# Hybrid stream encoder, first mixer: three transposes moved from TensorE to VectorE's 32x32 squares and DRAM

## The chip, the cores and the metric

One core of one Trainium2 chip. The metric is the device time of one execution in microseconds (us). The kernel before takes 1324.58 us, the median of 3 runs (1324.56 to 1324.66).

## The reference

One inference step of a two-layer encoder on 256 prompt frames and 32 sample frames (288 columns together), model width 1024, float32. Each layer is SwiGLU, mixer, SwiGLU, each behind an RMS norm and added to the stream. Layer 0's mixer, which the change is about, has 8 HGRN2 heads and 8 stick-breaking heads of 128 channels:

```python
def _mixer_ab(h, w_in, lb, g_out, g_q, g_k, w_out, s0, k_past, v_past):
    qa, fa, va, ga, qb, kb, vb = jnp.split(h @ w_in, ..., axis=-1)
    f = lb + (1.0 - lb) * jax.nn.sigmoid(fa)
    o_a, s_new = _hgrn2(silu(qa), 1.0 - f, va, jnp.log(f), s0)
    o_a = _rms(o_a, g_out) * jax.nn.sigmoid(ga)
    ...
    o_b = _stick_breaking(qb, pos, kb, vb, pos)
    return concat(o_a, o_b) @ w_out, s_new, kb, vb
# HGRN2:          S_t = diag(f_t) S_{t-1} + k_t v_t^T,  o_t = S_t^T q_t
# stick-breaking: A[t,s] = sigmoid(z_ts) * prod_{s<j<t} (1 - sigmoid(z_tj)),  o = A v
```

Layer 1's mixer is a gMLP; it and the four SwiGLU blocks are the same in both kernels.

## The kernel before, in words

Activations lie with channels on partitions and the 288 frames as columns. The weights stream from DRAM in chunks of 1024 rows x 256 columns (`fetch`, line 193, issued by SyncE's queue three chunks ahead into 3 buffers). ScalarE rounds each chunk to its high part `wh` (line 220), VectorE takes the rest `wl` (line 221), both in pieces of two 128-row blocks, four pieces to a chunk, and TensorE multiplies each block three times (`wl`, `wh` by the low part, `wh` by the high part: lines 260 to 262), 48 products of 288 columns to a chunk. A chunk's pieces are made while the chunk before it is multiplied. Where a chunk is complete, VectorE takes it out of PSUM (`evac`, `evac_heads`, lines 307 to 318).

The mixer (`mixer_ab`) takes four pairs of heads, numbered 0 to 3; each has seven chunks, in the order f, q, v, g, bv, bk, bq (HGRN's decay, query, value and gate, then stick-breaking's value, key and query). Small work runs beside the chunks in two lanes of Python generators: `hgrn` for a pair starts behind its v chunk, `stick_keys` behind bk, `stick` behind bq. `tick`, called after each 128-row block of a chunk, gives each lane its rate of steps (`RATES`), and a step runs to the next `yield`. At the end of the four pairs two output chunks are multiplied, the lanes are drained, and the last blocks follow. The Python order is only what the framework's scheduler starts from: it writes out one fixed queue for each engine, and each engine then works its queue strictly in that order, waiting where an operand or a buffer is not there. So the place of an instruction in its queue is decided when the program is built.

`hgrn` first makes the decayed products for seven levels (1, 2, 4 to 64 frames). At each level `widen` (lines 616, 617) updates `E` and `Pp`, `products` (596 to 600) writes a `QK` buffer (2 of them), TensorE makes the scores (623 to 628) and `place` (633, 639, 645) puts them into `sc` and `SS`; each level needs the one before. Then the decayed keys `kd` (tile `tmp`, lines 676, 677) are turned to frames-on-partitions by TensorE (`to_tok`, lines 142, 144, tile `kt`), the states `S` and outputs `o` are multiplied (696 to 718), ScalarE sums the squares (720), GpSimd takes the power (134), ScalarE scales (731), TensorE turns the outputs back (`to_cols`, lines 158, 160, tile `oT`) and VectorE gates them (740). `stick` makes scores `zs`, `z`, sigmoids, a scan on VectorE (858), the weights `Bz`, and turns them by TensorE (872 for the sample, 883 in `turned` for the prompt) before they multiply the values (895 to 901, tile `ob`).

`to_rows` (line 168 and line 172) already exists: VectorE turns each 32x32 square (`STREAM_TRANSPOSE`), four DMAs write the squares to a DRAM tile in row order, and a further DMA reads them back turned. Before, it is used for v and bv alone.

Of the kernel before, what the change touches and what calls it, by code (L numbers as in the profile page):

```python
# [22 lines left out]
PAST = 256
# [12 lines left out]
S2 = 2 * TS  # L36
N2 = 2 * NT
# [56 lines left out]
class Net:  # L94
    PIECE = 2
    NORM_RATE = 0.17
    RATES = (0.65, 0.55)

    def __init__(self, tc, ctx, I, O):
        self.tc, self.nc, self.I, self.O = tc, tc.nc, I, O  # L100
        e = ctx.enter_context
        self.const = e(tc.tile_pool(name="const", bufs=1))
        self.wraw = e(tc.tile_pool(name="wraw", bufs=3))
        self.wspl = e(tc.tile_pool(name="wspl", bufs=4))
        self.acc = e(tc.tile_pool(name="acc", bufs=2, space=PSUM))
        self.misc = e(tc.tile_pool(name="misc", bufs=4, space=PSUM))
        self.nrm = e(tc.tile_pool(name="nrm", bufs=1))
        self.rows = e(tc.tile_pool(name="rows", bufs=2, space=bass.MemoryType.DRAM))
        self.stream, self.pos = [], 0
        self.raw, self.spl = {}, {}  # L110
        self.uid = 0
        self.ahead = None
        self.lanes = []
        self.lv = None
        self.nlane = Lane(self.NORM_RATE)
# [418 lines left out]
    def hgrn(self, p, pool, d):  # L534
# [3 lines left out]
        nc, I, O = self.nc, self.I, self.O  # L538
        tt, mul = nc.vector.tensor_tensor, ALU.mult
# [8 lines left out]
        for b in range(2):  # L548
            h = 2 * p + b
            for x in (f[:, TS * b:TS * b + TS], f[:, S2:].rearrange("p (w h t) -> p h w t", w=2, h=2)[:, b]):  # L550
                nc.vector.tensor_scalar(out=x, in0=x, scalar1=self.lbc[:, h:h + 1],
                                        scalar2=self.lb[:, h:h + 1], op0=mul, op1=ALU.add)
        k = T("k")
# [12 lines left out]
        vs = vt[:, 0]  # L566
# [113 lines left out]
        Sn = T("Sn", [P, 2, 2, P])  # L680
        kts = []
        for b in range(2):
            pk = self.to_tok(kd, b, "kt")
            kt = T("kt", [P, 2, P], 2)
            nc.scalar.copy(out=kt, in_=pk[:, :TP].rearrange("p (w c) -> p w c", c=P))
            if b == 0:
                for h in range(2):
                    r = slice(TS * h, TS * h + TS)
                    nc.scalar.copy(out=ktz[r, h], in_=pk[r, TP:TP + P])
            kts.append(kt)  # L690
            yield
        for b in range(2):
            kt = kts[b]
            pn = self.ps("S")
            for w, (x, y) in enumerate(((kt[:, 0], vw(b)[:, 0]), (kt[:, 1], vw(b)[:, 1]), (ktz[:, b], vs))):
                mm(pn[:, w * P:w * P + P], lhsT=x, rhs=y, start=True, stop=True)  # L696
# [7 lines left out]

        g = d["g"]
        nc.scalar.activation(out=g, in_=g, func=AF.Sigmoid)
        po = []
# [18 lines left out]
        yield  # L726
        yield
        for b in range(2):
            on = T("on", [P, 384])
            for w in range(3 - b):  # L730
                nc.scalar.activation(out=on[:, w * P:w * P + P], in_=po[b][:, w * P:w * P + P], func=AF.Copy,
                                     scale=rs[:, 3 * b + w:3 * b + w + 1])
            yield
            pt = self.to_cols("oT", b, on[:, :TP].rearrange("p (w c) -> p w c", c=P), on[:, TP:])
            parts = [(b, slice(TS, NT), pt[:, :TP])]
            if b == 0:
                parts += [(h, slice(0, TS), pt[:, TP + TS * h:TP + TS * h + TS]) for h in range(2)]
            for h, c, x in parts:
                go = self.gc["go"] + 2 * p + h
                nc.vector.scalar_tensor_tensor(out=g[:, h, c], in0=x, scalar=self.cols[:, go:go + 1],  # L740
                                               in1=g[:, h, c], op0=mul, op1=mul)
            yield
        self.put(2 * p, g)
# [59 lines left out]
    def stick(self, p, pool, d):  # L803
# [75 lines left out]

        def turned(b):  # L880
            pw = self.ps("wT")
            for i in range(3):
                nc.tensor.transpose(pw[:, i * P:i * P + P], B[b][:, i * P:i * P + P], self.ident)
            wT = T("wT", [P, 384])
            nc.scalar.copy(out=wT, in_=pw[:, :384])
            return wT

        wT = turned(0)
        yield
# [6 lines left out]
        store(slice(kk, kk + 2), slice(0, TS), po[:, 0:S2].rearrange("p (h t) -> p h t", h=2))  # L896
        yield
        for b in range(2):
            po = self.ps("ob")
            mm(po[:, 0:256], lhsT=vt[:, 1 + b], rhs=wT[:, 0:256], start=True, stop=False)  # L900
            mm(po[:, 128:256], lhsT=vt[:, 3 + b], rhs=wT[:, 256:384], start=False, stop=True)
            if b == 0:
                wT = turned(1)
            store(kk + b, slice(TS, NT), po[:, :TP])
            yield
# [476 lines left out]
```

## Time and profile before

| | |
|---|---|
| runs | 1324.58 us median (1324.56 to 1324.66) |
| the profiled execution | 1324.58 us by the clock of the runs; span from first to last instruction 1322.9 us |
| TensorE busy | 1317.1 us, 100% of the span |
| VectorE, ScalarE, GpSimd busy | 887.1, 661.7, 41.7 us (67%, 50%, 3%) |
| mean DMA | 166 GB/s, 219.83 MB |
| mixer of layer 0 | about 222 to 497 us of the span |

TensorE's busy time counts the tail of each product, so its share says that it is never long without work, not that each product is at its peak rate. The other engines have idle time all along; what they do matters where TensorE's queue waits for it.

### The profile page before, as it was taken

The numbers are of one execution on the slowest core, as the hardware profiler recorded it, in microseconds if no ns is written. First come the engines' busy times: TensorE is split into PE (matmuls) and PEld (weight loads), VectorE is DVE, ScalarE is ACT, GpSimd is POOL, SyncE is SP. The second block draws the span as 40 slices with busy tenths as digits, with TensorE's granted clock in tenths as the row PEclk, the third lists the DMA queues.
The fourth block names the chain that finished last, engine by engine and source line by source line (L and its number), as shares of the span: only waits on it lengthen the run. The fifth ranks groups of instructions, "written<-read, shape, count | busy, mean of one in ns | idle before, by whom it ended". The sixth has DMA issues, their size and how long they took to land.

```text
span 1322.9 us, 24562 instructions
## 1 busy us (share of the span) xinstructions
PE 1317.1 (100%) x9922; PEld 1310.3 (99%) x9922; DVE 887.1 (67%) x1706; ACT 661.7 (50%) x1355; POOL 41.7 (3%) x70
## 2 busy tenths in 40 slices
PE   9999999999999999999999999999999999999998
PEld 9999999999999999999999999999999999999998
DVE  7666556889898866666655756655567976666653
ACT  7544445464746465544444644444655446444432
POOL 1000000010101000000000000030000000000000
PEclk9999999999999999999999999999999999999999
DMA  9555455565565546555545555576544545555453
GB/s 283 178 176 168 150 175 173 157 182 159 168 170 170 140 134 200 161 178 166 157 153 174 165 179 165 161 183 188 169 152 138 167 147 160 173 166 171 152 152 84
DMA packets 254852, 219.83 MB, mean 166 GB/s; under 512 B 41233, under 2 KB 254018, under 8 KB 254738
## 3 DMA queue, kind: packets, MB, share of 16 engines
q1 hardware_dynamic: 253906, 216.32, 53.5%
q0 software_dynamic: 672, 1.77, 0.7%
q8 instruction: 78, 1.28, 0.4%
q10 hardware_dynamic: 160, 0.17, 0.1%
q14 instruction: 36, 0.29, 0.1%
HBM read 210.89 MB, written 7.34 MB: 165 GB/s over the span
## 4 chain that ended last, share of the span: by engine, by line
PE 97%; DVE 2%; ACT 0%; issue 0%; POOL 0%; DVEq 0%
PE acc L262 30%; PE acc L261 30%; PE acc L260 30%; PE sc L623 1%; DVE wl L221 1%; PE sp L1082 1%; PE S L696 0%; PE zs L833 0%; PE acc L1157 0%; PE sc L651 0%; PE ob L900 0%; PE vt L988 0%; PE acc L280 0%; PE z L845 0%; PE ob L895 0%
## 5 line engine op out<-in xcount | busy, mean ns | idle before, releaser
L220 ACT CAST wh<-wraw 128x512 fp32r<-128x512 f32 x768 | 440.5, 619 | 490.3 <-PE acc L262 370.1
L221 DVE TENSOR_TENSOR wl<-wraw,wh 128x512 fp32r<-128x512 f32 x768 | 507.4, 688 | 253.4 <-ACT wh L220 252.9
L260 PE MATMUL acc<-xh,wl 128*128 128x288 f32 x2096 | 627.2, 299 | 0.0
L261 PE MATMUL acc<-xl,wh 128*128 128x288 f32 x2096 | 619.4, 295 | 0.0
L262 PE MATMUL acc<-xh,wh 128*128 128x288 f32 x2096 | 618.9, 295 | 0.0
L261 PEld LDWEIGHTS acc<-xl,wh 128*128 128x128 f32 x2096 | 394.1, 188 | 0.6
L260 PEld LDWEIGHTS acc<-xh,wl 128*128 128x128 f32 x2096 | 393.9, 188 | 0.4
L262 PEld LDWEIGHTS acc<-xh,wh 128*128 128x128 f32 x2096 | 393.6, 188 | 0.2
L260 PE MATMUL acc<-hh,wl 128*128 128x288 f32 x960 | 284.5, 297 | 0.0
L261 PE MATMUL acc<-hl,wh 128*128 128x288 f32 x960 | 283.4, 295 | 0.0
L262 PE MATMUL acc<-hh,wh 128*128 128x288 f32 x960 | 282.8, 295 | 0.0
L260 PEld LDWEIGHTS acc<-hh,wl 128*128 128x128 f32 x960 | 180.2, 188 | 0.8 <-DVE xT L402 0.2
L261 PEld LDWEIGHTS acc<-hl,wh 128*128 128x128 f32 x960 | 180.3, 188 | 0.1
L262 PEld LDWEIGHTS acc<-hh,wh 128*128 128x128 f32 x960 | 180.3, 188 | 0.0
L309 DVE TENSOR_TENSOR u<-acc,rb 128x576 f32<-128x576 f32 x52 | 39.3, 757 | 48.8 <-PE acc L262 48.8
L309 DVE TENSOR_TENSOR g<-acc,rb 128x576 f32<-128x576 f32 x47 | 35.6, 757 | 47.0 <-PE acc L262 47.0
L329 ACT CAST hh<-u 128x576 fp32r<-128x576 f32 x52 | 35.1, 675 | 58.4 <-DVE u L455 40.3
L330 DVE TENSOR_TENSOR hl<-u,hh 128x576 fp32r<-128x576 f32 x52 | 39.4, 758 | 7.1 <-ACT hh L329 1.3
L336 ACT ACTIVATE xh<-xT,cols 128x288 fp32r<-128x288 f32 x40 | 21.2, 531 | 24.8 <-DVE xT L404 15.4
L455 DVE TENSOR_TENSOR u<-u,g 128x576 f32<-128x576 f32 x44 | 33.1, 752 | 0.0
L453 ACT ACTIVATE g<-g 128x576 f32<-128x576 f32 x44 | 30.0, 682 | 0.1
L404 DVE SCALAR_TENSOR_TENSOR xT<-acc,xT 128x288 f32<-128x288 f32 x32 | 14.5, 455 | 17.0 <-PE acc L262 17.0
(303 smaller groups left out, 759.1 us busy)
## 6 DMA issues: line engine op xcount, KB each, us to landing
wraw<-in_ffn_w_up_dram SPq DMA_DIRECT2D x44, 1024.0 KB, 5.9
wraw<-in_ffn_w_gate_dram SPq DMA_DIRECT2D x43, 1024.0 KB, 5.4
wraw<-in_ffn_w_down_dram SPq DMA_DIRECT2D x32, 1024.0 KB, 5.7
wraw<-in_ab_w_in_dram SPq DMA_DIRECT2D x28, 1024.0 KB, 5.0
wraw<-in_c_w_in_dram SPq DMA_DIRECT2D x16, 1024.0 KB, 5.5
wraw<-in_ffn_w_down_dram SPq DMA_DIRECT2D x16, 768.0 KB, 4.6
wraw<-in_c_w_out_dram SPq DMA_DIRECT2D x8, 1024.0 KB, 5.6
wraw<-in_ab_w_out_dram SPq DMA_DIRECT2D x8, 768.0 KB, 5.2
```

The lines of the kernel that those rows point to most:

```text
L220: self.nc.scalar.copy(out=h[:, x], in_=w[:, a:b])
L221: self.nc.vector.tensor_tensor(out=l[:, x], in0=w[:, a:b], in1=h[:, x].bitcast(F32), op=ALU.subtract)
L260: mm(o, lhsT=l[:, k, c], rhs=hi[:, r], start=st, stop=False)
L261: mm(o, lhsT=h[:, k, c], rhs=lo[:, r], start=False, stop=False)
L262: mm(o, lhsT=h[:, k, c], rhs=hi[:, r], start=False, stop=en)
L309: self.nc.vector.tensor_tensor(out=x, in0=acc[:, :, :NT], in1=self.rb, op=ALU.mult)
L329: nc.scalar.copy(out=hh, in_=h)
L330: nc.vector.tensor_tensor(out=self.hl[:, k:k + 2], in0=h, in1=hh.bitcast(F32), op=ALU.subtract)
L336: nc.scalar.activation(out=self.xh[:, k], in_=x, func=AF.Copy, scale=g)
L404: nc.vector.scalar_tensor_tensor(out=x, in0=acc[b][:, :NT], scalar=scale, in1=x, op0=ALU.mult, op1=ALU.add)
L453: nc.scalar.activation(out=g, in_=g, func=AF.Silu)
L455: nc.vector.tensor_tensor(out=u, in0=u, in1=g, op=ALU.mult)
```

## The change

Everything is in layer 0's mixer.

- `hgrn`: the decayed keys `kd` go through `to_rows` (one VectorE transpose of 576 columns, four writes) and come back by one read into `kt` and two into `ktz`, in place of five TensorE transposes and four ScalarE copies for each pair. Seven `yield`s stand between the issue and the first use. The sigmoid of the gate moves ahead of them.
- `hgrn`: the prompt's normalised outputs go through `to_rows` (512 columns) and come back into the buffer of `vt`; the sample's part keeps one TensorE transpose, so four fewer for each pair. Seven more `yield`s stand before the gating.
- `stick`: the prompt's weights of both heads go through `to_rows` (384 columns each, turned in the key buffer `kn`) and come back into `wT` and into the buffer `pk` of the past keys, in place of six TensorE transposes and two ScalarE copies for each pair. Seven more `yield`s.
- The decay's floor, `lb + (1 - lb) * sigmoid`, four operations for each pair, moves from VectorE to ScalarE (line 551).
- DRAM row tiles: 6 buffers in place of 2. Lane rates: 0.85 and 0.62 in place of 0.65 and 0.55.

```diff
-    RATES = (0.65, 0.55)
+    RATES = (0.85, 0.62)
...
-        self.rows = e(tc.tile_pool(name="rows", bufs=2, space=bass.MemoryType.DRAM))
+        self.rows = e(tc.tile_pool(name="rows", bufs=6, space=bass.MemoryType.DRAM))
...
-                nc.vector.tensor_scalar(out=x, in0=x, scalar1=self.lbc[:, h:h + 1],
-                                        scalar2=self.lb[:, h:h + 1], op0=mul, op1=ALU.add)
+                nc.scalar.activation(out=x, in_=x, func=AF.Identity, scale=self.lbc[:, h:h + 1],
+                                     bias=self.lb[:, h:h + 1])
...
-        kts = []
-        for b in range(2):
-            pk = self.to_tok(kd, b, "kt")
-            kt = T("kt", [P, 2, P], 2)
-            nc.scalar.copy(out=kt, in_=pk[:, :TP].rearrange("p (w c) -> p w c", c=P))
...
+        kt = T("kt", [P, 4, P])
+        rows = self.to_rows(T("QK", [P, S2 + N2], 2)[:, 0:N2], [(0, kd)])
+        nc.sync.dma_start(out=kt, in_=rows[S2:].rearrange("(i t) c -> t i c", t=P))
+        for h in range(2):
+            r = slice(TS * h, TS * h + TS)
+            nc.sync.dma_start(out=ktz[r, h], in_=rows[r])
+        g = d["g"]
+        nc.scalar.activation(out=g, in_=g, func=AF.Sigmoid)
+        for _ in range(7):
+            yield
...
-            pt = self.to_cols("oT", b, on[:, :TP].rearrange("p (w c) -> p w c", c=P), on[:, TP:])
...
+        rows = self.to_rows(T("QK", [P, S2 + N2], 2)[:, 0:4 * P], [(0, on)])
+        ot = T("vt", [P, 5, P])
+        nc.sync.dma_start(out=ot[:, 0:4], in_=rows.rearrange("(i c) t -> c i t", c=P))
+        yield
+        pt = self.ps("oT")
+        nc.tensor.transpose(pt[:, 0:P], os, self.ident)
...
+        for _ in range(7):
+            yield
+        for h in range(2):
+            gated(h, slice(TS, NT), ot[:, 2 * h:2 * h + 2].rearrange("p w t -> p (w t)"))
...
-        wT = turned(0)
+        wTs = []
+        y = T("kn", [P, 2 * (PAST + NT)])
+        for b in range(2):
+            wT = T(("wT", "pk")[b], ([P, 384], [P, 2, PAST])[b])
+            wT = wT if b == 0 else wT.rearrange("p h s -> p (h s)")[:, 0:384]
+            rows = self.to_rows(y[:, 384 * b:384 * b + 384], [(0, B[b])])
+            nc.sync.dma_start(out=wT.rearrange("p (i t) -> p i t", t=P), in_=rows.rearrange("(i s) t -> s i t", s=P))
+            wTs.append(wT)
...
-        yield
+        for _ in range(7):
+            yield
         for b in range(2):
             po = self.ps("ob")
+            wT = wTs[b]
             mm(po[:, 0:256], lhsT=vt[:, 1 + b], rhs=wT[:, 0:256], start=True, stop=False)
             mm(po[:, 128:256], lhsT=vt[:, 3 + b], rhs=wT[:, 256:384], start=False, stop=True)
-            if b == 0:
-                wT = turned(1)
```

The change also moves instructions in the queues that the scheduler writes. Three places, where numbers tell tiles of one name apart, `acc` is a chunk's sum in PSUM, `wl` and `wh` are a chunk's low and high part, and `E`, `f`, `QK`, `sc`, `SS` belong to the levels of `hgrn`.

VectorE, from the end of pair 1's bq chunk to the first piece of pair 2's f chunk (`wl_4006` before, `wl_3902` in the change). Before:

```order
L781 TENSOR_SCALAR ks_3936<-kms_3935 128x5
L221 TENSOR_TENSOR wl_4006<-wraw_3768,wh_4005 128x512
L317 TENSOR_TENSOR bq_3993<-acc_3866,rb_2579 128x2x2x128
L786 SCALAR_TENSOR_TENSOR bkt_3899<-kt_3937,pw_3987,gk_2528 128x128 x3
L318 TENSOR_TENSOR bq_3993<-acc_3866,rb_2579 128x64
L786 SCALAR_TENSOR_TENSOR bkt_3899<-kt_3962,pw_3987,gk_2528 128x128 x2
L221 TENSOR_TENSOR wl_4006<-wraw_3768,wh_4005 128x512
```

There the levels of pair 1 are over when bq is taken out, and a piece of the next chunk stands ahead of it. In the change the queue goes on like this behind bq (the first rows, then the last):

```order
L317 TENSOR_TENSOR bq_4014<-acc_3892,rb_2579 128x2x2x128
L617 TENSOR_TENSOR f_3343<-f_3343 128x144x2
L596 TENSOR_TENSOR QK_3687<-k_3584,E_3591 128x40x4
L597 TENSOR_TENSOR QK_3687<-k_3584,E_3591 128x2x16x4
L598 TENSOR_TENSOR QK_3687<-q_3449,f_3343 128x256
L600 TENSOR_TENSOR QK_3687<-q_3449,f_3343 128x8x4
L883 TENSOR_TENSOR hl_2511<-ob_3708,hh_2510 128x256
```

```order
L639 COPY_PREDICATED SS_2518<-ls,sc_3808 64x64
L616 TENSOR_TENSOR E_3591<-E_3591,f_3343 128x4x64
L673 TENSOR_TENSOR qz_2519<-q_3449,f_3343 128x2x32
L617 TENSOR_TENSOR f_3343<-f_3343 128x4x64
L676 TENSOR_TENSOR tmp_3886<-k_3584,E_3591 128x320
L674 TENSOR_TENSOR q_3449<-q_3449,f_3343 128x256
L677 TENSOR_TENSOR tmp_3886<-k_3584,E_3591 128x2x128
L221 TENSOR_TENSOR wl_3902<-wraw_3673,wh_3901 128x512
```

From bq up to and with the first `wl` for pair 2's f chunk there are 45 instructions (rows with x2 counted twice), and no piece of the f chunk stands ahead of them.

TensorE at the same place: `acc_3892` is pair 1's bq chunk, `acc_4017` pair 2's f chunk. Before, one level of pair 1 and what follows it:

```order
L262 MATMUL acc_3866<-xh,wh_3776 128x288
L623 MATMUL sc_3931<-QK_3857 128x128 x2
L142 MATMUL kt_3937<-ident,bk_3863 128x128 x2
L144 MATMUL kt_3937<-ident,bk_3863 128x128
L260 MATMUL acc_3866<-xh,wl_3828 128x288
L261 MATMUL acc_3866<-xl,wh_3827 128x288
L262 MATMUL acc_3866<-xh,wh_3827 128x288
L260 MATMUL acc_3866<-xh,wl_3828 128x288
```

The level's scores stand among products of a chunk there, 18 products to a level. In the change:

```order
L908 MATMUL ob_3708<-pk_3508,bvt_3110 128x128
L623 MATMUL sc_3738<-QK_3687 128x128 x2
L623 MATMUL sc_3773<-QK_3723 128x128 x2
L626 MATMUL sc_3773<-QK_3723 128x128
L623 MATMUL sc_3808<-QK_3753 128x128 x2
L628 MATMUL sc_3808<-QK_3753 128x64
L623 MATMUL sc_3834<-QK_3785 128x128 x2
L623 MATMUL sc_3865<-QK_3820 128x128 x2
L142 MATMUL kt_3965<-ident,bk_3889 128x128 x2
L144 MATMUL kt_3965<-ident,bk_3889 128x128
L142 MATMUL kt_3982<-ident,bk_3889 128x128 x2
L260 MATMUL acc_4017<-xh,wl_3902 128x288
```

Six levels of scores (the first, `sc_3704`, just ahead of the rows shown), the second head of pair 0's `ob` and pair 1's key transposes now stand in a row between the last product of one chunk and the first of the next, with no product between them.

ScalarE, pair 1's outputs `o` and their norm (`on`, `so`, `pw`), up to the copy that the sample's transpose `oT` reads. Before:

```order
L547 ACTIVATE f_4141<-f_4141 128x576
L720 ACTIVATE on_4098,so_4099<-o_4135 128x128
L825 ACTIVATE bq_3993<-bq_3993,cols 128x512
L819 ACTIVATE on_4119,qms_4120<-ss_4122 128x128 x2
L614 COPY E_4398<-f_4141 128x288
L819 ACTIVATE on_4119,qms_4120<-ss_4122 128x128
L819 ACTIVATE on_4119,qms_4120<-ss_4157 128x128
L220 CAST wh_4273<-wraw_3997 128x512
```

In the change, pair 2's outputs:

```order
L797 COPY kn_4774<-kn_4915 128x256
L824 ACTIVATE on_4943,qms_4944<-ss_4946 128x128
L830 ACTIVATE bq_4841<-bq_4841,cols 128x512
L824 ACTIVATE on_4943,qms_4944<-ss_4946 128x128
L556 ACTIVATE tmp_5240<-q_5103 128x576
L824 ACTIVATE on_4943,qms_4944<-ss_4946 128x128
L824 ACTIVATE on_4943,qms_4944<-ss_4970 128x128 x2
L220 CAST wh_5115<-wraw_4845 128x512
L731 ACTIVATE on_4982<-o_4905,pw_4960 128x128
L220 CAST wh_5115<-wraw_4845 128x512
L220 CAST wh_5176<-wraw_4845 128x512 x2
```

The last scaled copy (L731, formerly one of the first three behind the power) now stands behind the copies of `kn`, the squares of stick-breaking's query, the scaling of bq, the sigmoid of the next q and a piece of the next chunk.

## Rows read from the trace of the kernel before

**Rows 1.** The page: busy time by engine, granted TensorE clock in 40 slices.

```profile
PE 1317.1 (100%) x9922; PEld 1310.3 (99%) x9922; DVE 887.1 (67%) x1706; ACT 661.7 (50%) x1355; POOL 41.7 (3%) x70
...
PEclk9999999999999999999999999999999999999999
```

**Rows 2.** Windows: one half of a pair; us, busy time (instructions) by engine, clock, DMA.

```profile
252.00:283.00 31.00, 30.82 (x241) 30.09 (x240) 27.81 (x81) 14.43 (x47) 2.08 (x3) 1.00 0.45 133
```

**Rows 3.** TensorE in order of time: start, duration, line, tiles, shape, count.

```profile
482.29 0.30 PE L262 MATMUL acc<-hh,wh 128*128 128x288 f32 x1
482.42 0.49 PE L872 MATMUL wTs<-ident,Bsz 128*128 128x128 f32 x3
482.75 0.49 PE L883 MATMUL wT<-ident,Bz 128*128 128x128 f32 x3
482.99 0.38 PE L260 MATMUL acc<-hh,wl 128*128 128x288 f32 x1
483.21 0.30 PE L261 MATMUL acc<-hl,wh 128*128 128x288 f32 x1
```

**Rows 4.** VectorE's groups by shape: busy us, mean ns of one, idle before.

```profile
L221 DVE TENSOR_TENSOR wl<-wraw,wh 128x512 fp32r<-128x512 f32 x768 | 507.4, 688 | 253.4 <-ACT wh L220 252.9
L598 DVE TENSOR_TENSOR QK<-q,f 128x256 f32<-128x256 f32 x28 | 11.6, 413 | 0.0
L633 DVE COPY_PREDICATED sc<-lv,sc 128x256 f32<-128x256 uint8 x20 | 11.1, 557 | 0.4
L617 DVE TENSOR_TENSOR f<-f 128x288 f32<-128x288 f32 x20 | 9.2, 461 | 0.1
L858 DVE TENSOR_TENSOR_SCAN C<-C,cfr 128x384 f32<-128x384 f32 x8 | 8.6, 1073 | 0.1
L616 DVE TENSOR_TENSOR E<-E,f 128x288 f32<-128x288 f32 x16 | 7.2, 452 | 0.0
L597 DVE TENSOR_TENSOR QK<-k,E 128x128 f32<-128x128 f32 x24 | 6.8, 284 | 0.0
L596 DVE TENSOR_TENSOR QK<-k,E 128x160 f32<-128x160 f32 x16 | 5.2, 325 | 0.0
L639 DVE COPY_PREDICATED SS<-ls,sc 64x64 f32<-64x64 uint8 x20 | 4.5, 224 | 0.1
L858 DVE TENSOR_TENSOR_SCAN Cs<-Cs,cfr 64x288 f32<-64x288 f32 x4 | 3.0, 750 | 2.5 <-ACT Cs L836 2.5
L317 DVE TENSOR_TENSOR bq<-acc,rb 128x512 f32<-128x512 f32 x4 | 2.7, 677 | 0.0
```

**Rows 5.** The chain that ended last: start, us, engine, tile, line, instructions.

```profile
303.70 0.43 PE ob L900 x2
...
311.88 0.44 PE sc L623 x4
```

**Rows 6.** ScalarE's groups by shape, 222 to 500 us.

```profile
L731 ACT ACTIVATE on<-o,pw 128x128 f32<-128x128 f32 x20 | 6.1, 375 | 0.1
...
L720 ACT ACTIVATE on<-o 128x128 f32<-128x128 f32 x20 | 5.5, 274 | 10.3 <-PE o L718 9.4 <-PE o L714 0.6
...
L720 ACT ACTIVATION_READ_ACCUMULATOR on<-o 128x1 f32 x20 | 3.9, 194 | 0.0
...
L556 ACT ACTIVATE tmp<-q 128x576 f32<-128x576 f32 x4 | 2.8, 688 | 0.0
```

**Rows 7.** GpSimd's groups by shape: the power behind the sums of squares.

```profile
L134 POOL TENSOR_TENSOR pw<-oms,mhalf 128x5 f32<-128x5 f32 x4 | 5.1, 1268 | 45.0 <-DVE oms L724 45.0
```

**Rows 8.** DMA issues by line: count, KB each, median us from issue to landing.

```profile
rows<-QK SPq DMA_DIRECT2D x16, 80.0 KB, 2.1
vt<-rows SPq DMA_DIRECT2D x4, 320.0 KB, 4.6
```

**Rows 9.** TensorE in order of time at the start of the span.

```profile
1.16 3.36 PE L1157 MATMUL acc<-ones 128*128 128x128 f32 x14 [1.16 <-DVE ms L1168]
...
8.69 0.82 PE L1193 MATMUL x<-ident,xs 128*128 128x128 f32 x6
```

More of the change, by code (lines that the diff above doesn't have):

```diff
@@ L680, in hgrn @@
         Sn = T("Sn", [P, 2, 2, P])
-        kts = []
-        for b in range(2):
-            pk = self.to_tok(kd, b, "kt")
-            kt = T("kt", [P, 2, P], 2)
-            nc.scalar.copy(out=kt, in_=pk[:, :TP].rearrange("p (w c) -> p w c", c=P))
-            if b == 0:
[L687 to L690, printed above, removed]
+        kt = T("kt", [P, 4, P])
[7 more added lines that the diff above has]
+        for _ in range(7):
             yield
         for b in range(2):
-            kt = kts[b]
             pn = self.ps("S")
-            for w, (x, y) in enumerate(((kt[:, 0], vw(b)[:, 0]), (kt[:, 1], vw(b)[:, 1]), (ktz[:, b], vs))):
+            for w, (x, y) in enumerate(((kt[:, b], vw(b)[:, 0]), (kt[:, 2 + b], vw(b)[:, 1]), (ktz[:, b], vs))):
                 mm(pn[:, w * P:w * P + P], lhsT=x, rhs=y, start=True, stop=True)
@@ L703, in hgrn @@
             nc.sync.dma_start(out=o[0, 0, 2 * p:2 * p + 2].rearrange("h c d -> c h d"), in_=Sn[:, w])
-        g = d["g"]
-        nc.scalar.activation(out=g, in_=g, func=AF.Sigmoid)
         po = []
@@ L727, in hgrn @@
         yield
+        on, os = T("tmp")[:, 0:4 * P], T("on", [P, 384])[:, 0:P]
         for b in range(2):
-            on = T("on", [P, 384])
-            for w in range(3 - b):
-                nc.scalar.activation(out=on[:, w * P:w * P + P], in_=po[b][:, w * P:w * P + P], func=AF.Copy,
+            for w in range(2):
+                c = slice((2 * b + w) * P, (2 * b + w) * P + P)
+                nc.scalar.activation(out=on[:, c], in_=po[b][:, w * P:w * P + P], func=AF.Copy,
                                      scale=rs[:, 3 * b + w:3 * b + w + 1])
-            yield
-            pt = self.to_cols("oT", b, on[:, :TP].rearrange("p (w c) -> p w c", c=P), on[:, TP:])
[L735 to L741, printed above, removed]
-            yield
+        nc.scalar.activation(out=os, in_=po[0][:, TP:384], func=AF.Copy, scale=rs[:, 2:3])
+        rows = self.to_rows(T("QK", [P, S2 + N2], 2)[:, 0:4 * P], [(0, on)])
[4 more added lines that the diff above has]
+        nc.tensor.transpose(pt[:, 0:P], os, self.ident)
+        gated = lambda h, c, x: nc.vector.scalar_tensor_tensor(
+            out=g[:, h, c], in0=x, scalar=self.cols[:, self.gc["go"] + 2 * p + h:self.gc["go"] + 2 * p + h + 1],
+            in1=g[:, h, c], op0=mul, op1=mul)
+        for h in range(2):
+            gated(h, slice(0, TS), pt[:, TS * h:TS * h + TS])
+        for _ in range(7):
+            yield
+        for h in range(2):
+            gated(h, slice(TS, NT), ot[:, 2 * h:2 * h + 2].rearrange("p w t -> p (w t)"))
+        yield
         self.put(2 * p, g)
@@ L878, in store @@
             nc.vector.tensor_tensor(out=self.hl[:, k, t], in0=x, in1=self.hh[:, k, t].bitcast(F32), op=ALU.subtract)
[L880 to L886, printed above, removed]
-        wT = turned(0)
+        wTs = []
[6 more added lines that the diff above has]
+            wTs.append(wT)
         yield
@@ L896, in stick @@
         store(slice(kk, kk + 2), slice(0, TS), po[:, 0:S2].rearrange("p (h t) -> p h t", h=2))
-        yield
+        for _ in range(7):
+            yield
         for b in range(2):
             po = self.ps("ob")
+            wT = wTs[b]
             mm(po[:, 0:256], lhsT=vt[:, 1 + b], rhs=wT[:, 0:256], start=True, stop=False)
             mm(po[:, 128:256], lhsT=vt[:, 3 + b], rhs=wT[:, 256:384], start=False, stop=True)
-            if b == 0:
-                wT = turned(1)
             store(kk + b, slice(TS, NT), po[:, :TP])
```

## The prediction, made before the changed kernel was run

> **What bounds the kernel now.** I read the page first: TensorE is busy for 1317.1 of 1322.9 us and its granted clock is full in every slice [rows 1]. In the order of time its products follow each other without a hole: one product of 288 columns takes 0.13 us of its queue [rows 3]. So a microsecond of TensorE's work that goes is a microsecond gained, and a microsecond in which TensorE waits is lost. The windows come next, since they show who could make it wait: in this half of a pair VectorE is busy for 27.8 of 31 us, ScalarE for 14.4 [rows 2]. VectorE has 10% to spare there, and it makes the low part of the weights for every product.
>
> **What goes.** 64 transposes (16 a pair: 5 of the keys, 5 of the outputs, 6 of the weights, 15 net of the one that stays) become 4: 60 fewer. In the order of time six of them and the product behind them take 482.42 to 483.21, 0.79 us; less 0.13 for the product, 0.66 / 6 = 0.11 us each [rows 3]. 60 x 0.11 = **6.5 us** off the path, 0.5%. ScalarE's copies out of PSUM that go and VectorE's four floor operations a pair are off TensorE's path; I cost them at nothing.
>
> **What comes, off the path.** Four VectorE transposes a pair and 22 more DMA issues on SyncE's queue. A write of rows lands in 2.1 us, the read back in 4.6 [rows 8], so a round trip is about 7 us with its issues. In the new TensorE queue keys, outputs and weights are first used 12 us or more of products behind their issue, so I expect no wait for a landing before pair 3's last weights. The next weights stand behind these issues on the same queue, but are fetched three chunks, some 19 us, ahead.
>
> **What comes, on the path.** The rows of order decide: the queues are fixed, and the new ones no longer mix the levels of `hgrn` with the pieces of the weights.
>
> (a) Behind bq of pairs 1, 2 and 3. VectorE has 45 instructions from the taking out of bq up to the first `wl` of the next chunk. By shape [rows 4]: bq 0.68; five L616, three at 0.452 and two of 256 columns at 0.41 (as L598), 2.18; six L617, 2.66; the products of three levels, 0.325 + 0.284 + 0.413 and L600 at 0.22 (as the small L639), 3.73; of two levels, 0.98 each, 1.96; four L633, 2.23; five L639, 1.12; `hl` 0.41; the last four about 1.5; `wl` 0.69. Sum 17.2 us, all behind the last product of bq. TensorE has in that time six scores of 0.44, three smaller ones of 0.22, one `ob` of 0.65 [rows 5] and five transposes of 0.11: 4.5 us. It waits 12.7 us, three times: **38.1**.
>
> (b) bk is taken out ahead of the first `wl` of bq (0.68 + 0.22 + 0.69 = 1.6), and in front of bv stand a `place` and a `wl` behind a score (0.56 + 0.69 = 1.25) [rows 4]; three pairs: **8.5**.
>
> (c) The norm of the outputs. ScalarE's queue from o's first head to the copy that `oT` reads: five squares of 0.47, 2.3, with VectorE's mean 0.2 and the power 1.27 [rows 7], four scaled copies of 0.375, 1.5, three of `kn`, 1.1, five squares, 2.3, bq's scaling and q's sigmoid at 0.69, one `wh` at 0.69, the copy 0.375: 11.1 us [rows 6]. TensorE has 45 products, the rest of o and five transposes, 7.4 us. It waits 3.7. Then the sample's weights: power, two pieces, a scan of 0.75, a piece and four small operations on VectorE, some 4.9 us against 3.5 on TensorE, 1.4 more. Three pairs x 5.1 = 15.3; pair 3 has only 19 products to put between, wait 7.2 + 0.5 = 7.7. Sum **23.0**.
>
> (d) Pair 0's levels are still mixed with products, but with about 11 to a level, not 18: from the second to the last score VectorE has, by the same prices and with one `wl` and bv's taking out, 14.9 us, TensorE 65 products (8.6) and five scores (2.9), 11.5. It waits 3.4; bk, taken out behind that, comes 1.1 late by the same count: **4.5**.
>
> (e) The end. Between the sample's weights and the last blocks TensorE has 4.5 us; VectorE has two scans of 1.07 and their products and transposes, five pieces, the gating, then ScalarE's rounding: 9.5. Wait 5.0. The second weight round trip (two more issues and a read behind the first) adds 3.5: **8.5**.
>
> (f) A product's result comes about 0.16 us after its slot: the last three transposes end at 483.24, their slots at 483.08 [rows 3]. At some 20 such places: **3.4**.
>
> Waits 38.1 + 8.5 + 23.0 + 4.5 + 8.5 + 3.4 = 86.0; less 6.5: +79.5. The profiled execution took 1324.58 us, 1322.9 of it span, which is also the median of the runs; so 1324.6 + 79.5 = 1404.1, I say **1404**.
>
> Unseen operations. A transpose of 384 columns lies between nothing saved and the 0.69 of a `wl`; four floor operations on ScalarE between 0.2 and 0.69 each; both stand inside waits already counted or off the path, so between 0 and 2 us in all; I take 0, as they are nearest to work that is hidden now. A landing at 4.6 us rather than 2.1 moves (e) by 2.5.
>
> TensorE's clock, apart from this sum: at the start of the span 14 products of 128 columns take 3.36 us, 0.24 each, where four such passes take 0.44, 0.11 each, later; they follow 1.16 us of no work, and the close spacing is there at 8.69, six transposes in 0.82 [rows 5, 9]. So the lower level, 1.2 GHz by this spacing, is a state of this kernel too, at its start; from 8.69 on it is 2.4. The waits of (a) are the first long idleness of TensorE after that. The Trainium skill, "TensorE: Matmul & The Clock Gate", Part 1 (The HAM clock gate), says that an idle TensorE falls back to half rate and must be busy again before it gets the full one. The trace's start agrees, and no row shows a fall in the middle. By the rule the change would lose more than the waits; that is a rival below.
>
> **Rivals.**
> 1. The clock falls in each wait of (a). Price from the start: 1.16 to 8.69 at half rate loses 3.8 us; three times, 11: **1415**. For it: 12.7 us of waits with short scores only. Against: it may come back sooner, and what follows a wait may be held by VectorE anyway.
> 2. Only (a), (b) and (f) are waits, since in (c) to (e) ScalarE and VectorE run ahead in the idle time that (a) gives them: 38.1 + 8.5 + 3.4 - 6.5 = +43.5, **1368**. For it: they do work while TensorE stands. Against: the queues of (c) begin at o, which TensorE must first make.
> 3. SyncE becomes late. The load of the past keys into `pk` now waits for pair p's second `ob`, at the end of (a)'s start, and pv, the key rows and the next g chunk's weights stand behind it. If each pair's g chunk came 10 us late: +30, **1434**. It decides from the point where the 22 issues and their landings use up the 19 us of lead.
> 4. Not slower: VectorE reaches the levels early, while bq is multiplied, and only (b) and small waits stay, below the 6.5 us that are saved: **1318**. The place is (a): if bq's taking out did not stand ahead of the levels, or waits there came to under 2.2 us each. The rows of order speak against it, and nothing of the profile for it.
> 5. The edit does not do what it says: TensorE would still turn. Order shows 60 transposes fewer; I give it nothing.
>
> **How the numbers follow.** The forecast 0.45 (its own range 1388 to 1420, by 20% of the waits), rival 1 0.27, rival 2 0.15, rival 3 0.09, rival 4 0.04. 1365 to 1438 holds all but rival 4 and the half of rival 3 that goes beyond. 0.2% (2.6 us) is about what a measurement of this kernel can tell from no change. Slower 0.96, within 0.2% 0.01, faster 0.03.
>
> **What would show it.** In the new profile TensorE's sum of product groups is 6.5 us less and its idle time some 85 us more. The largest idle group stands before the first low product of a chunk, released by VectorE's `wl`, with three waits of about 13 us. Idle time before `oT` is put down to ScalarE's `on`, before `wTs` to VectorE's `Bsz`. If rival 1 holds, products behind the long waits stand twice as far apart, 0.27 us. If idle time before `S`, `ob` or the weights' pieces is put down to DMAs, rival 3 holds. The prediction is wrong if TensorE's waits before `wl` sum to under 25 us, or if the span grows by under 40.

## The result, and the profile after

The changed kernel takes 1385.45 us, the median of 4 runs (1385.08 to 1386.12), beside 1324.57 us for the kernel before on the same chip: ratio 1.046, 95% interval 1.0442 to 1.0478. It is slower by 60.9 us; the forecast was +79.5. 1385.45 lies inside the range of 1365 to 1438, and 2.6 us below the forecast's own of 1388 to 1420.

The page of the changed kernel answers to [rows 1]: 60 instructions of TensorE fewer, a span of 1383.4 us, and granted clock below full in some slices of the mixer.

```profile
span 1383.4 us, 24560 instructions
...
PE 1334.0 (96%) x9862; PEld 1318.4 (95%) x9862; DVE 892.8 (65%) x1706; ACT 660.4 (48%) x1347; POOL 43.6 (3%) x70
...
PEclk9999999999998988999999999999999999999999
```

By busy time TensorE's idle time grew by 43.6 us only (1383.4 - 1334.0 against 1322.9 - 1317.1), since a product at half rate counts as busy for longer. So I count otherwise: from the start of one TensorE instruction to the start of the next, less the slot that its kind takes in an undisturbed stretch (0.1325 us a product, 0.11 a transpose, other kinds likewise). In the mixer (222 to 560 us) that leaves 70.5 us of loss, where the kernel before has 3.0 (222 to 545). The difference, 67.4, less the 6.5 us of the 60 transposes is 60.9: the whole change of the time lies here.

Who ended TensorE's waits, over the whole span of the changed kernel (engine, tile and line that waited, who came last: us in all, times, longest):

```profile
PE acc L260 <- DVE wl L221: 12.8, 10, 3.2
PE sc L623 <- DVE QK L600: 9.5, 6, 1.9
PE ss L142 <- ACT tmp L729: 6.0, 4, 1.7
PE wTs L877 <- DVE Bsz L869: 4.3, 3, 1.5
PE acc L260 <- ACT hh L329: 3.9, 1, 3.9
PE sc L623 <- DVE SS L639: 3.7, 3, 1.2
PE sc L623 <- DVE QK L598: 2.7, 6, 0.6
...
```

The six groups left out are of 1.2 us and less. No wait is put down to a DMA. TensorE in order of time behind bq of pair 1, in the changed kernel:

```profile
333.92 0.30 PE L262 MATMUL acc<-xh,wh 128*128 128x288 f32 x1
334.05 0.61 PE L623 MATMUL sc<-QK 128*128 128x128 f32 x4
...
338.71 0.68 PE L623 MATMUL sc<-QK 128*128 128x128 f32 x4 [1.86 <-DVE QK L600]
...
345.56 1.20 PE L623 MATMUL sc<-QK 128*128 128x128 f32 x4 [1.24 <-DVE SS L639]
...
348.07 0.61 PE L260 MATMUL acc<-xh,wl 128*128 128x288 f32 x1 [0.25 <-DVE wl L221]
...
349.19 0.45 PE L261 MATMUL acc<-xl,wh 128*128 128x288 f32 x1
349.43 0.45 PE L262 MATMUL acc<-xh,wh 128*128 128x288 f32 x1
```

14.0 us from the first score to the next chunk's first product, for 4.5 us of slots: 9.5 lost. Then the products stand 0.24 apart, not 0.13, for 12 starts: 1.3 more. VectorE has no hole in the same stretch, no gap above 0.04 us:

```profile
334.25 0.69 DVE L317 TENSOR_TENSOR bq<-acc,rb 128x512 f32<-128x512 f32 x1 [3.73 <-PE acc L262]
334.86 0.45 DVE L617 TENSOR_TENSOR f<-f 128x288 f32<-128x288 f32 x1
335.22 0.32 DVE L596 TENSOR_TENSOR QK<-k,E 128x160 f32<-128x160 f32 x1
335.46 0.28 DVE L597 TENSOR_TENSOR QK<-k,E 128x128 f32<-128x128 f32 x1
...
347.33 0.68 DVE L221 TENSOR_TENSOR wl<-wraw,wh 128x512 fp32r<-128x512 f32 x1
347.94 0.76 DVE L168 STREAM_TRANSPOSE QK<-tmp 128x576 f32<-128x576 f32 x1
```

Nearly every instruction starts before the recorded end of the one ahead of it: L617 is 0.45 long, and the next starts 0.36 behind its start.

### The profile page after: what moved, and what is told of

The parts are those of the page before. It is cut to its first block, busy times and chain, and to the rows that moved or that the text cites. A ratio compares the mean times of both kernels' runs of the same rounds, so it can differ in the third digit from the quotient of the medians.

```text
span 1383.4 us, 24560 instructions
## 1 busy us (share of the span) xinstructions
PE 1334.0 (96%) x9862; PEld 1318.4 (95%) x9862; DVE 892.8 (65%) x1706; ACT 660.4 (48%) x1347; POOL 43.6 (3%) x70
## 4 chain that ended last, share of the span: by engine, by line
PE 90%; DVE 5%; ACT 2%; issue 1%; POOL 1%; DMA 0%; SPq 0%; DVEq 0%; ACTq 0%
PE acc L260 29%; PE acc L261 29%; PE acc L262 29%; DVE wl L221 1%; POOL pw L134 1%; PE sp L1087 1%; DVE f L617 0%; DVE E L616 0%; DVE sc L633 0%; PE S L694 0%; PE sc L623 0%; DVE QK L598 0%; PE acc L1162 0%; PE sc L651 0%; PE vt L993 0%
## 5 line engine op out<-in xcount | busy, mean ns | idle before, releaser
L623 PE MATMUL sc<-QK 128*128 128x128 f32 x112 | 24.0, 349 | 15.9 <-DVE QK L600 9.5
L623 PEld LDWEIGHTS sc<-QK 128*128 128x128 f32 x112 | 19.0, 239 | 19.7 <-issue 14.1
L882 ACT CAST hh<-ob 128x256 fp32r<-128x256 f32 (+1 forms) x12 | 3.8, 319 | 62.9 <-PE ob L908 55.8
```

What stands on the lines that cost most here:

```text
L623: mm(ps[:, b * P:b * P + P], lhsT=X[:, col(0, b)], rhs=X[:, B2].rearrange("p (w h t) -> p w h t", w=2, h=2)[:, :, b], start=True, stop=True)
```

## The experiments

First, for the sections below, TensorE's queue as built: how many products of chunks stand between the scores of one level and those of the next, pair 1, levels 1 to 7 (the order of time in the traces gives the same counts), with each time (medians) less that of the kernel before on the same chip.

| kernel | products between the levels | us | difference |
|---|---|---|---|
| before | 18 18 18 18 18 18 | 1324.57 | |
| change | 144 0 0 0 0 0 | 1385.45 | +60.9 |
| rates alone | 41 11 11 13 10 20 | 1327.56 | +3.1 |
| floor alone | 18 18 18 18 18 18 | 1324.56 | 0.0 |
| weights alone | 87 6 10 15 11 3 | 1345.03 | +20.6 |
| keys alone | 23 13 18 18 24 18 | 1334.95 | +10.4 |
| outputs alone | 18 18 18 18 24 18 | 1327.49 | +2.9 |
| change, old rates | 48 0 0 0 0 12 | 1408.34 | +83.9 |
| change, weights' DMAs on ScalarE's queue | 78 3 11 16 10 13 | 1384.64 | +60.2 |
| change, outputs by TensorE | 144 0 0 0 0 0 | 1378.69 | +54.1 |
| change, waits filled | 144 0 0 0 0 0 | 1382.27 | +57.7 |

Line numbers of a variant are its own. The theory: the time goes where the new queue order puts mixer work in a row without products between; rivals: the rates, the landings of the round trips, the clock.

**The rates alone.**

```diff
-    RATES = (0.65, 0.55)
+    RATES = (0.85, 0.62)
```

> The kernel before with nothing but the two lane rates of the change (0.85, 0.62): all 64 transposes stay on TensorE. In TensorE's queue the levels then stand 10 to 13 products apart instead of 18, in all four pairs, as pair 0's levels do in the changed kernel, and none stand in a row without products. Theory (the time went where levels were moved behind bq): small waits only, about 2.4 us a pair as in pair 0 of the changed kernel, so 1324.6 + 4 x 2.4 = 1334, between 1326 and 1340. Rival (the rates are the cause): at least half of the 60.9 us, 1355 or more.

1327.56 us (ratio 1.0024, 1.0014 to 1.0034). That is inside the range expected, below its 1334: the largest single loss in the mixer is 0.26 us. With the other parts in, the rates even help: the change with the old rates is 23 us slower. They are not the cause.

**The change with the old rates.**

```diff
-    RATES = (0.85, 0.62)
+    RATES = (0.65, 0.55)
```

> The changed kernel with the old lane rates (0.65, 0.55). In TensorE's queue S, o and the norm of the outputs of pair 1 then stand some 120 products further back, three and five levels of pair 1 stand in a row around the key transposes, pair 2's levels are mixed with products, and pair 3's last five levels stand in a row with S, o, the weights and the blocks at the very end. Theory (order decides): the waits of pair 2 behind bq go, those of pair 1 stay, and the end gets a long one of 20 to 40 us: 1385.4 - 11 + 20 to 40, about 1405, between 1385 and 1430. Rival (the rates cost the time): back to 1320 to 1335.

1408.34 us (1.0631, 1.0615 to 1.0647), close to the forecast by the order: five losses of 1.0 to 1.8 in front of pair 1's scores, and at the end 17.3 us in front of `S`, where decayed keys, round trip and states stand behind each other with no products left; 17.0 of it is put down to the landing of the keys' read. Some 21 us more, which the forecast had not placed, stand in nine losses before the products of chunks; the largest, 6.4, is put down to VectorE's taking out of `g`. That the lane must take the added steps somewhere is my reading, not tested.

**The weights alone** (the change's part in `stick`, with six row buffers; all else as before).

```diff
-        wT = turned(0)
+            rows = self.to_rows(y[:, 384 * b:384 * b + 384], [(0, B[b])])
+            nc.sync.dma_start(out=wT.rearrange("p (i t) -> p i t", t=P), in_=rows.rearrange("(i s) t -> s i t", s=P))
```

> The kernel before with only the stick-breaking prompt weights turned by VectorE and DRAM, old rates, floor on VectorE: 24 transposes fewer, -2.6 us. In TensorE's queue the third level's scores of pairs 1 to 3 move back by some 70 to 85 products, the later levels stand 10 to 15 apart and the last one or two in a row with the key transposes. Theory: the weights' DMAs alone displace the levels, and as only the tail is in a row each pair loses 3 to 8 us: 1322 + 9 to 24, about 1338. Rival (it takes keys and outputs too): 1322, within 1 us. Rival (landings are late): idle time of TensorE before ob put down to DMAs, 5 us a pair or more.

1345.03 us (1.0157, 1.014 to 1.0174): at the upper end. The weights' part alone pushes the levels back; which of its pieces does it (the DMAs, the squares on VectorE, the six more steps) this run does not tell apart. In front of `sc` it loses up to 1.8 us a time, and at the end 1.7 and 4.9 us in front of `ob`, put down to landings: there the rival on landings holds, since nothing is left to cover them.

**The keys alone** (the change's part on `kt`, `ktz`).

```diff
-            pk = self.to_tok(kd, b, "kt")
+        rows = self.to_rows(T("QK", [P, S2 + N2], 2)[:, 0:N2], [(0, kd)])
+        nc.sync.dma_start(out=kt, in_=rows[S2:].rearrange("(i t) c -> t i c", t=P))
```

> The kernel before with only the decayed keys turned by VectorE and DRAM, old rates: 20 transposes fewer, -2.2 us. In TensorE's queue the levels stay mixed with products, but S, o and the stick-breaking scores z of each pair now stand in one row without products between them, some 75 to 90 products later. Theory (an order in rows costs): TensorE waits there for ScalarE's copy of S and the squares, 2 to 5 us a pair, no wait behind bq: 1322.3 + 8 to 20, about 1335. Rival (only displaced levels cost): 1322.3, within 2 us.

1334.95 us (1.0079, 1.0065 to 1.0092), as expected in time, but not in place: no wait is put down to ScalarE's copy of `S`. The largest waits are before `oT`, on ScalarE's `on`, 5.3 us in four, the longest (2.9) at the end, where `oT` follows `o` without a product between. So not only displaced levels cost.

**The floor alone** (four operations a pair from VectorE to ScalarE).

```diff
-                nc.vector.tensor_scalar(out=x, in0=x, scalar1=self.lbc[:, h:h + 1],
+                nc.scalar.activation(out=x, in_=x, func=AF.Identity, scale=self.lbc[:, h:h + 1],
```

> The kernel before with only decay's floor moved from VectorE to ScalarE: four operations a pair. TensorE's queue differs only by two products at zs. Theory (both lie beside TensorE's work): 1324.5, within 0.4 us. Rival (the longer chain on ScalarE delays f and with it the first level): 1326 or more.

1324.56 us (0.9999, 0.9991 to 1.0008): nothing, as the prediction took it. The five parts alone add up to +37.0; together they cost 60.9. The other 24 us come of their company: no part alone puts six levels in a row.

**The weights' DMAs on another queue.** The change, with the work on every engine the same.

```diff
-            rows = self.to_rows(y[:, 384 * b:384 * b + 384], [(0, B[b])])
-            nc.sync.dma_start(out=wT.rearrange("p (i t) -> p i t", t=P), ...)
+            rows = self.to_rows(y[:, 384 * b:384 * b + 384], [(0, B[b])], nc.scalar)
+            nc.scalar.dma_start(out=wT.rearrange("p (i t) -> p i t", t=P), ...)
```

> The changed kernel, with the ten DMAs of the weights' two round trips of each pair issued on ScalarE's queue instead of SyncE's; the same work on every engine, the same round trips. In TensorE's queue the levels of pairs 1 to 3 then have 10 to 16 products between them again from the third level on, and the last stands 7 products ahead of the key transposes. Theory (the fixed order alone makes the waits behind bq): those waits go, three times some 10 us and about 1 us of half clock: 1385.4 - 3 x 11 = 1352, between 1345 and 1362; the waits in front of ss and wTs stay. Rival (the round trips themselves are late): no gain, 1380 or more, with TensorE's idle time before the same products.

1384.64 us (1.0455, 1.0439 to 1.0471). The time says rival, the place says theory: over the scores behind bq, where the changed kernel loses 9.5, this one loses 1.7 (325 to 344 us). But 5.2 to 5.9 us a pair are lost earlier, and 8.9 at the end. TensorE, then ScalarE with its queue of DMAs (ACTq), then a window (us, busy time and instructions by engine, clock, DMA share, GB/s):

```profile
317.70 1.22 PE L623 MATMUL sc<-QK 128*128 128x128 f32 x4 [5.05 <-ACT QK L594]
```

```profile
309.09 1.13 ACTq L172 DMA_DIRECT2D rows<-kn  x2
...
312.14 0.34 ACT L593 COPY QK<-k 128x160 f32<-128x160 f32 x1
316.92 0.38 ACTq L892 DMA_DIRECT2D pk<-rows  x1
317.34 0.31 ACT L594 COPY QK<-k 128x128 f32<-128x128 f32 x1 [4.86 <-DMA S<-in_state_hgrn_dram]
```

```profile
312.00:317.00 5.00, 0.65 (x5) 0.41 (x4) 1.77 (x3) 0.48 (x2) 0.00 (x0) 0.86 1.00 300
```

The read `pk<-rows` stands in ScalarE's queue and by the program needs its row writes, which land while the DMA engines are full (share 1.00). Behind it stands L594, a copy for level 1; the DMA that the row names is only the last that landed ahead of it. The Trainium skill, "DMA: Bandwidth & Descriptors", section Issuing engines are not separate DMA queues, says that another issuing engine only saves sequencer time. Here it also moved a wait of some 4.5 us (312.48 to 316.92) from SyncE, whose queue holds DMA issues alone, to an engine on TensorE's path. My forecast of 1352 fell by that.

**The outputs by TensorE again, in the change.**

```diff
-        rows = self.to_rows(T("QK", [P, S2 + N2], 2)[:, 0:4 * P], [(0, on)])
+            pt = self.to_cols("oT", b, on[:, :TP].rearrange("p (w c) -> p w c", c=P), on[:, TP:])
```

> The changed kernel with the prompt outputs turned by TensorE again (16 more transposes, +1.8 us); keys, weights, rates and floor as in the change. In TensorE's queue the levels of pairs 1 to 3 still stand in a row behind bq. The prediction's term (c), 23 us, laid to the outputs' norm on ScalarE's queue: if the outputs' new way makes it, 1385.4 + 1.8 - 15 to 23, about 1368. Theory (the norm's copies are the same either way, and the waits in front of the query's transposes stand for PSUM that those copies free): they stay, 1385.4 + 1.8, between 1380 and 1390.

1378.69 us (1.041, 1.0394 to 1.0426): 6.8 us less though 1.8 us of transposes came back. My theory here fell, the prediction's term (c) stands at less than half its size: the wait before `ss` (6.0 us in the changed kernel) is gone, that before `wTs` falls from 4.3 to 0.7, while at the end `ob` waits 3.0 for landings.

**The waits filled.** Work added, nothing moved.

```diff
+            if p > 0 and 0 < i < 6:
+                for _ in range(6):
+                    mm(ps[:, 384:512], lhsT=self.ident, rhs=self.ident, start=True, stop=True)
             return ps
```

> The changed kernel, with six more products of 128 columns (the identity by itself, into unused columns of the scores' PSUM tile) behind the scores of levels 2 to 6 of pairs 1 to 3; the order of everything else is the same. They fill TensorE's waits for VectorE with 1.3 us of work each time. Theory (VectorE sets the time there, the clock only adds what half rate costs after the wait): where the clock stays full, the products behind the wait stand 0.13 apart from the first on and the scores and key transposes are twice as fast: 1 to 2 us less a pair, 1380 to 1383, though 15 x 1.3 = 20 us of work was added. Rival (the clock costs nothing that VectorE does not hide): 1385 to 1386. Rival (VectorE is not what TensorE waits for): up to 20 us more.

1382.27 us (1.0436, 1.042 to 1.0452): 3.2 us faster with 20 us more work. The two intervals overlap, but the runs do not: 1382.1 to 1382.4 here, 1385.1 to 1386.1 for the change. TensorE behind the same wait as above:

```profile
348.30 0.40 PE L260 MATMUL acc<-xh,wl 128*128 128x288 f32 x1 [1.28 <-DVE wl L221]
...
348.67 0.29 PE L262 MATMUL acc<-xh,wh 128*128 128x288 f32 x1
348.80 0.29 PE L260 MATMUL acc<-xh,wl 128*128 128x288 f32 x1
```

The chunk starts when VectorE is done, 348.30 as against 348.07, and VectorE's 45 instructions take 13.8 us in both, so VectorE sets that place. The products stand 0.13 apart at once. The clock's price in (a) is 3.2 / 3 = 1.1 us a pair; the two falls at the end, where nothing was filled, are there in both. Windows of the changed kernel, then of this one:

```profile
334.00:340.00 6.00, 3.15 (x22) 2.55 (x20) 5.67 (x19) 4.43 (x9) 0.23 (x1) 1.00 0.22 36
341.00:350.00 9.00, 6.93 (x27) 6.11 (x28) 8.92 (x28) 3.17 (x16) 0.58 (x1) 0.50 0.13 38
351.00:357.00 6.00, 6.00 (x47) 6.00 (x46) 4.56 (x12) 2.31 (x6) 1.32 (x1) 1.00 0.53 110
416.00:429.00 13.00, 10.27 (x40) 9.15 (x41) 12.34 (x38) 4.82 (x20) 1.72 (x2) 0.50 0.25 52
494.50:504.00 9.50, 6.47 (x26) 5.35 (x26) 9.39 (x31) 2.80 (x14) 0.00 (x0) 0.50 0.15 36
```

```profile
333.00:348.00 15.00, 13.40 (x110) 12.63 (x109) 13.36 (x45) 6.21 (x19) 0.63 (x2) 1.00 0.24 58
```

**The outputs alone, three ways.** Here the order seemed to cost nothing, so a gain was in reach.

```diff
+            on, os = T("tmp")[:, 0:4 * P], T("on", [P, 384])[:, 0:P]
...
+            rows = self.to_rows(T("QK", [P, S2 + N2], 2)[:, 0:4 * P], [(0, on)])
```

> The kernel before with only the prompt outputs turned by VectorE and DRAM, old rates: 16 transposes fewer, 16 x 0.11 = -1.8 us. TensorE's queue stays mixed everywhere: 6 to 18 products between every two pieces of the mixer. Theory (nothing but the order costs): 1322.7, between 1322.3 and 1324. Rival (a DRAM round trip costs by itself, some 1 us a pair or more): 1326 or more.

1327.49 us (1.0023, 1.0014 to 1.0032): slower, and by time in the rival's range. By place it is not: three losses of 0.8 to 1.5 us, none on a DMA, 3.3 in sum; less the 1.8 saved they give 1.5 of the 2.9 us, and the rest stays open. Next, pair 3 as before and three steps in place of seven:

```diff
+        if p < HB // 2 - 1:
...
-        for _ in range(7):
+            for _ in range(3):
```

> The kernel before with the prompt outputs of pairs 0 to 2 turned by VectorE and DRAM, and three steps of the lane between the read and its use instead of seven, so that the generator takes nearly as many steps as before; pair 3, rates, floor, keys and weights as before. 12 transposes fewer, 12 x 0.11 = -1.3 us. The pieces of the mixer stand in TensorE's queue as in the kernel before, up to a few products, in all four pairs. Theory (the order makes the loss, not the round trip): 1323.2, between 1322.9 and 1324, a little faster than both kernels; the run with seven steps had 1327.5. Rival (a round trip costs about 1 us a pair whatever the order): 1326 or more.

1326.27 us (1.0012, 1.0003 to 1.0021). TensorE has three losses of 1.03 us, all before `zs`:

```profile
PE zs L859 <- ACT on L845: 2.6, 3, 0.9
```

```profile
285.60 0.27 ACT L845 ACTIVATE on<-ss 128x128 f32<-128x128 f32 x1
...
286.71 0.37 ACT L734 ACTIVATE tmp<-o,pw 128x128 f32<-128x128 f32 x1 [0.76 <-POOL pw L134]
```

ScalarE now scales the outputs in between the query's squares, and waits for GpSimd's power there. 12 transposes save 1.3 us, three waits lose 3.1: +1.8, measured +1.7, so nothing is left for the round trip, though the time is in its rival's range again. Last, the scaled copies put back behind the squares by their tile:

```diff
-            on, os = T("tmp")[:, 0:4 * P], T("on", [P, 384])[:, 0:P]
+            on = T("on", [P, 640])
+            on, os = on[:, 0:4 * P], on[:, 4 * P:]
```

> As the run in step (outputs of pairs 0 to 2 turned by VectorE and DRAM, three steps), but the scaled copies of the outputs go to the tile on, widened to 640 columns, instead of tmp; that tile also takes the squares of the query, so ScalarE's queue has the scaled copies behind those squares again, as in the kernel before, where the run in step has them in between. 12 transposes fewer, -1.3 us. Theory (order on ScalarE made the three waits of 1.03 us in front of zs): those go, 1323.2, between 1322.8 and 1323.8, faster than both kernels by 0.1%. Rival (the round trips cost something of their own): the waits in front of zs go, but the time stays at 1324.5 or more.

1327.16 us (1.0021, 1.0012 to 1.003). The waits before `zs` went and came back in front of the sample's transpose, whose copy now stands behind the sample's sigmoids:

```profile
PE oT L743 <- ACT on L737: 2.7, 3, 0.9
```

The sum gives +1.8 again; the span grew by 2.0, the median by 2.6, and the difference stays open. So the rival's time (1324.5 or more) came true and its reason was not shown. A version without either wait, 1323.2 by the sum, was not run.

**Outputs, and weights of pairs 0 to 2 on GpSimd's queue.**

```diff
+            rows = self.to_rows(y[:, 384 * b:384 * b + 384], [(0, B[b])], nc.gpsimd)
+            nc.gpsimd.dma_start(out=wT.rearrange("p (i t) -> p i t", t=P), ...)
```

> The kernel before with the prompt outputs turned by VectorE and DRAM, and the stick-breaking weights of pairs 0 to 2 too, with the weights' ten DMAs a pair on GpSimd's queue; keys, pair 3's weights, rates and floor as before. 34 transposes fewer, 34 x 0.11 = -3.7 us. TensorE's queue has 6 to 18 products between all pieces of the mixer, as before. Theory (the order makes the loss, not the round trips): 1320.8, between 1320.3 and 1323, faster than both kernels. Rival (the reads that wait for their writes block the queue they stand on, here GpSimd's power and its copies of the sample's levels): TensorE waits for sc or for the norms, 1326 to 1340.

1338.41 us (1.0106, 1.0092 to 1.0119), the rival in time, not in place: not `sc` or the norms wait but `ob`, 7.5 us for landings, with the order as mixed as before. GpSimd in order of time, pair 0's two round trips:

```profile
299.44 3.75 POOL L172 DMA_DIRECT2D rows<-kn  x6 [3.26 <-DVE kn L168]
306.57 0.76 POOL L905 DMA_DIRECT2D wT<-rows  x1 [3.39 <-DMA rows<-kn]
307.32 1.25 POOL L172 DMA_DIRECT2D rows<-kn  x2
314.83 0.75 POOL L905 DMA_DIRECT2D pk<-rows  x1 [6.25 <-issue]
```

15.4 us from the first write to the second read. In the changed kernel SyncE needs 8.0 for the same pair:

```profile
303.48 4.40 SPq L172 DMA_DIRECT2D rows<-kn  x6
...
311.52 0.38 SPq L892 DMA_DIRECT2D pk<-rows  x1
```

The two do not differ in the queue alone: the DMA engines' mean share is 0.87 over 299 to 315 us here and 0.45 over 303 to 312 in the changed kernel. What each adds is not shown.

No version tried beats the kernel before.

## Why the prediction came out as it did

The sign and the mechanism were right: TensorE's loss is in the mixer, at the places that the rows of order named, but for (c) and (d). The size was 18.6 us too high: (a), (c), (d) and (f) together 24.7 too high, (b) and (e) 6.1 too low, so part of the error cancelled by luck. By terms, in us; measured is the loss by the count above:

| term | predicted | measured |
|---|---|---|
| (a) behind bq, three pairs | 38.1 | 10.8 + 11.4 + 10.2 = 32.4, of it some 3.2 the clock |
| (b) bk and bv | 8.5 | 9.9 (1.5 to 1.8 at each of six places) |
| (c) norm of the outputs | 23.0 | 11.4 |
| (d) pair 0's levels | 4.5 | none (2.4 in 222 to 290, of it 1.6 the first wait of (c); before 1.3) |
| (e) the end | 8.5 | 5.3 (524 to 532) + 7.9 (541 to 549) = 13.2, of it some 4 the clock |
| (f) result tails | 3.4 | 0.5 (the rest of 67.4; tails inside the waits are counted there) |

**The terms that were mis-sized.** In (a) the step "Sum 17.2 us" multiplied counts by the mean durations of [rows 4]. The 45 instructions took 13.8 us, 334.25 to 348.01, though their recorded durations sum to 16.8: where VectorE's queue is full, each overlaps the next by some 0.07 us. In the changed kernel it is 0.37 from start to start of 288 columns and 0.61 of 512, not the 0.461 and 0.688 of the rows. The kernel before shows it too: two `wl` in a row from 311.00 us take 1.28, so it could have been read ahead. The Trainium skill, "Vector Engine (DVE) Microarchitecture Reference", section 5.2 (Measured stream behaviour on trn2), has 1.0417 ns a column and about 75 ns an instruction; an estimate from these is 0.375 and 0.61 us, and the trace agrees. The 13.8 less TensorE's 4.5 leave 9.3, beside the 9.5 lost.

(c) was too large in part for the same reason, on ScalarE (its four scaled copies take 1.14 us in a row, not 1.5), and its place was wrong. `oT` never waits. What waits is `ss`, for PSUM that the scaled copies free, behind the power (TensorE, ScalarE, GpSimd of the changed kernel):

```profile
290.28 0.44 PE L142 MATMUL ss<-ident,bq 128*128 128x128 f32 x2 [1.41 <-ACT tmp L729]
```

```profile
289.08 1.14 ACT L729 ACTIVATE tmp<-o,pw 128x128 f32<-128x128 f32 x4 [1.48 <-POOL pw L134]
```

```profile
287.88 1.17 POOL L134 TENSOR_TENSOR pw<-oms,mhalf 128x5 f32<-128x5 f32 x1 [13.51 <-DVE oms L720]
```

1.57 us a pair here and some 1.6 before `wTs`, against 3.7 and 1.4. (d) fell away: VectorE keeps up with levels 10 to 13 products apart, as in the run with the rates alone, where all four pairs are spaced so and no loss is above 0.26.

(e) was too small, and by other parts. The 5.0 are right in kind: the gating stands behind five `wl` in VectorE's queue, and the rounding behind the gating, 4.1 us. The 3.5 for a second weight round trip were not paid in the change; in their place the products of the output chunk wait 3.3 us for a `wl` behind ScalarE's squares, and the clock falls twice. By the spacing of what runs at the lower clock there, that is some 4 us, an estimate; no run tests it. TensorE, then windows:

```profile
527.79 0.61 PE L260 MATMUL acc<-hh,wl 128*128 128x288 f32 x1 [3.15 <-DVE wl L221]
...
542.41 0.85 PE L260 MATMUL acc<-hh,wl 128*128 128x288 f32 x2 [3.93 <-ACT hh L329]
```

```profile
525.00:531.00 6.00, 3.21 (x9) 2.63 (x10) 2.54 (x7) 3.50 (x13) 1.64 (x1) 0.50 0.85 212
542.00:548.00 6.00, 4.89 (x16) 4.06 (x16) 1.52 (x3) 0.69 (x2) 0.00 (x0) 0.50 0.95 270
```

**The rivals.** Rival 1 was right that the clock falls in each wait of (a), and wrong by its price: 1.1 us a pair, not 3.8, since most of the half rate lies inside the wait. The 3.8 was itself too high: in the kernel before, two products take 0.54 us at 7.59, nearly what they take later (0.51 at 9.26), so half rate had ended before 8.69. And rival 1 did not look at the end, where the clock falls too. The clock went from 2.4 GHz to 1.2 between 340 and 341 us, behind scores with waits of 0.6 to 1.9 us between them, and stayed where the waits were filled. This agrees with the rule of "TensorE: Matmul & The Clock Gate", Part 1 (The HAM clock gate), in the Trainium skill, cited ahead. Rival 2 (1368) named too few places: (c) and (e) hold 24.6 us. Rival 3 does not hold in the change, where no wait is put down to a DMA; its sign, a wait before `S` or `ob` put down to landings, is there in five of the variants. Rivals 4 and 5 did not happen.

**The signs named.** I said that waits before `wl` of under 25 us in sum would prove me wrong; they are 12.8, of them 0.8 behind bq. By that sign (a) was wrong as I had stated it, with three waits of 13 us before one product; it is right in what TensorE waits for. Most of (a) stands before its scores, 15.9 us in the three rows of `sc`, put down to the same VectorE run: I had placed in front of one product what is spread over the scores. Before `wTs` it is `Bsz`, as named. TensorE's idle time was to grow by some 85 us and grew by 43.6, as said at the start.

What stays open: why the scheduler pushes the levels back is not shown by any run. Shown is that the weights' part alone puts 87 products between the first two levels, and that in the change, with the same DMAs on ScalarE's queue, the later levels are mixed again while 78 products still stand between the first two. What order does to time is shown for (a), by that run and by the filled waits; (b) and (e) are read from the trace alone.

## What to carry to other kernels

In this kernel, work off TensorE's path was free only while the queue order still had products to put around it; before making such a change, count the products between dependent steps in the new queue, and price a row of small instructions by start-to-start distances from a dense stretch. A read that waits for its own writes holds up what stands behind it on its queue, so keep it off the queue of an engine on TensorE's path; and five edits together cost more here than the sum of each alone. Twelve saved transposes, 1.3 us, are lost to three waits of one microsecond on an engine that only looks idle.

## What was not expected of the hardware

VectorE at a full queue: 13.8 us for 45 instructions whose recorded durations sum to 16.8. TensorE: 20 us of useless products made the kernel 3.2 us faster, because the granted clock stayed at 1.00 at three places where it had been 0.50. DMA: two round trips of the weights took 15.4 us to the issue of the second read on GpSimd's queue, and 8.0 on SyncE's, there with the DMA engines half as busy.
